# Nine unread products ahead of the first one, and input splits queued behind weight splits, in a hybrid SSM layer

## The chip, the cores and the metric

The kernel runs on one core of one Trainium2 chip. The metric is the device time of one execution in microseconds. Engines are named as in the profile: PE (TensorE, matmul), DVE (VectorE), ACT (ScalarE), POOL (GpSimd) and SP (SyncE, which issues most DMAs).

## The reference

One layer of a streaming encoder, for 256 prompt positions and 32 sample positions that share the weights. All data is f32.

```python
xn   = rmsnorm(x, norm_mix_pre)                  # x: 288 x 2048 in all
proj = xn @ w_in     # columns: u_pool 1024 | z 2048 | xBC 2560 | dt 32
pool = multi-scale trailing mean of u_pool, then a grouped product
ssd  = Mamba-2 mixer: causal conv on xBC, exact chunked scan, SiLU(z) gate, norm
x    = x + rmsnorm(concat[pool, ssd] @ w_out, norm_mix_post)
x    = x + rmsnorm(ConvFFN(rmsnorm(x, norm_ffn_pre)), norm_ffn_post)   # D_FF 5632
```

## The kernel before

The 288 positions are the columns of every product, and features lie on the 128 partitions. To get f32 accuracy from the faster f32r product, each operand is split into a high part (a copy rounded to f32r, on ACT) and a low part (the rest, on DVE). Each tile of 128 x 128 weights then costs three products, `mm3`: high weights by high input (L136), high weights by low input (L137), low weights by high input (L138).

The norm of the input is taken out of the product: the input is only scaled by the gain `g_mix_pre` while it is split (`split_from`, L99 on ACT and L100 on DVE), and `rstd` is multiplied in when the sums leave PSUM. `rstd` needs the sum of squares: ACT squares each input tile (L230 for the first, L233 into a `xsq` buffer for the others), POOL adds it to `xsum` (L234), and PE forms the mean with one product with the constant matrix `mean` (L242, into `prs`); ACT takes the root (L237) and DVE the reciprocal (L238).

The first stage runs over k, 16 steps of 128 input features. It forms 768 columns of `xBC` in six PSUM accumulators (five `acc`, one of the three `aux` banks), so a step is 6 x 3 = 18 products. Each step has one input split, one high weight split (L270, ACT) and one low weight split (L271, DVE). The weights come in DMAs of one or two steps from `w_first` into four `raw` buffers, and the split weights lie in four `whi` and four `wlo` buffers, so a split waits until PE has done with the step four earlier. SP issues the loads of input and weights in turn. After step 15 PE forms `dt` (`pdt`, L289), and the loops over the other `w_in` columns begin (`project`, with L130 and L131 as the weights' splits); there, DVE and ACT also do the convolutions and the scan, whose operands pass through DRAM (`xs_d`, `xw`, L450).

The order of instructions on an engine isn't written out: a scheduler places them by its own estimate of when each is ready, within the dependencies. `tc.keep_in_program_order` holds an instruction at its place in the program. `tc.issue_after(ins)` puts what is traced in its block behind `ins` on the engine of `ins`; it fixes the order of issue alone, and nothing waits for `ins` to end.

Of the kernel before, what the change touches and what calls it, by code (L numbers as in the profile page):

```python
# [8 lines left out]
F32 = mybir.dt.float32  # L9
F32R = mybir.dt.float32r  # L10
AF = mybir.ActivationFunctionType
# [5 lines left out]
P = 128  # L17
# [4 lines left out]
NT = NP_ + NS  # L22
# [21 lines left out]
def body(  # L44
# [26 lines left out]
    act, dve, pool, pe, sp = nc.scalar, nc.vector, nc.gpsimd, nc.tensor, nc.sync  # L71
# [11 lines left out]
    def aux(shape, name):  # L83
        return aux_ps.tile(shape, F32, tag="aux", name=name)

    def atile(name):
        return apool.tile([P, 2, NT], F32R, tag="a", name=name)
# [4 lines left out]
    def split_from(a, src, scale=None):  # L92

        if scale is None:
            act.activation(a[:, 0, :], src, AF.Copy)
            dve.tensor_tensor(a[:, 1, :], src, a[:, 0, :].bitcast(F32), op=ALU.subtract)
        else:
            return (
                act.activation(a[:, 0, :], src, AF.Copy, scale=scale),  # L99
                dve.scalar_tensor_tensor(  # L100
                    a[:, 1, :], src, scale, a[:, 0, :].bitcast(F32), op0=ALU.mult, op1=ALU.subtract
                ),
            )

    def wtile(part, n, nc_):

        t = wpool.tile([P, 1024 + 64], F32R, tag=part, name="w" + part)
        return t[:, 58 : 58 + n * nc_].rearrange("p (k c) -> p k c", k=n)
# [3 lines left out]
    def fetch_w(view, kb, nk, c0, nc_):  # L112
        raw = wpool.tile([P, nk, nc_], F32, tag="raw", name="raw")
        with tc.high_priority(offset=ahead[0]):
            sp.dma_start(out=raw, in_=view[:, c0 // 256, kb : kb + nk, :nc_])
        return raw
# [18 lines left out]
    def mm3(out, wh, wl, a, start, stop):  # L135
        pe.matmul(out, wh, a[:, 0, :], start=start, stop=False)  # L136
        pe.matmul(out, wh, a[:, 1, :], start=False, stop=False)  # L137
        pe.matmul(out, wl, a[:, 0, :], start=False, stop=stop)  # L138
# [43 lines left out]
    mean = const.tile([P, P], F32, name="mean")  # L182
# [29 lines left out]
    g_mix_pre = const.tile([P, KD], F32, name="g0")  # L212
# [5 lines left out]
    start = ExitStack()  # L218
    xin = start.enter_context(tc.tile_pool(name="xin", bufs=1))
    xT = xin.tile([P, KD, NT], F32, name="xT")  # L220
# [4 lines left out]
    def input_tiles(kb, n):  # L225
        sp.dma_start(out=xT[:, kb : kb + n, :], in_=x_in[:, kb : kb + n, :])

    def input_squares(k):
        if k == 0:
            act.activation(xsum, xT[:, k, :], AF.Square)  # L230
        else:
            q = xin.tile([P, NT], F32, tag="xsq", bufs=2, name="xsq")
            act.activation(q, xT[:, k, :], AF.Square)  # L233
            pool.tensor_tensor(xsum, xsum, q, op=ALU.add)  # L234

# [4 lines left out]
    def input_rstd():  # L240
        p_ = aux([P, NT], "prs")
        pe.matmul(p_, mean, xsum, start=True, stop=True)  # L242
        root(rstd, p_)

    act.dma_start(out=g_mix_pre, in_=g0_in)
    input_tiles(0, 1)
    first = [acc_ps.tile([P, NT], F32, tag="acc", name="acc") if m < 5 else aux([P, NT], "acc_x") for m in range(6)]
    chunks = ((0, 1), (1, 1)) + tuple((k, 2) for k in range(2, KD, 2))
    x_with = {0: (1, 1), 1: (2, 2), 2: (4, 2), 4: (6, 3), 6: (9, 3), 8: (12, 4)}
    for kb, n in chunks:  # L250
        raw = wpool.tile([P, n, 768], F32, tag="raw", name="raw")
        sp.dma_start(out=raw, in_=w_first[:, kb : kb + n, :])
        if kb in x_with:
            input_tiles(*x_with[kb])
        if kb == 1:
            pool.dma_start(out=wdt, in_=w_dt)
        if kb == 2:
            pool.dma_start(out=par1, in_=par1_in)
            pool.dma_start(out=hp, in_=hp_in)
        if kb == 6:  # L260
            pool.dma_start(out=pc, in_=par2_in[:, :120])
            pool.dma_start(out=pf, in_=par2_in[:, 120:].rearrange("p (r t) -> p r t", r=6))
        for k in range(kb, kb + n):
            a = atile("xn")
            split_from(a, xT[:, k, :], g_mix_pre[:, k : k + 1])
            xn.append(a)
            hi, lo = wtile("hi", 1, 768)[:, 0, :], wtile("lo", 1, 768)[:, 0, :]
            step = 256 if k == 0 else 768
            for c in range(0, 768, step):
                act.activation(hi[:, c : c + step], raw[:, k - kb, c : c + step], AF.Copy)  # L270
                dve.tensor_tensor(  # L271
                    lo[:, c : c + step], raw[:, k - kb, c : c + step], hi[:, c : c + step].bitcast(F32), op=ALU.subtract
                )
            for t in range(k - 1, k) if 0 < k < 9 else range(2 * k - 10, 2 * k - 8) if 8 < k < 13 else ():
                input_squares(t)
            if k == 13:
                input_rstd()
            for m in range(6):
                c = slice(m * P, (m + 1) * P)
                mm3(first[m], hi[:, c], lo[:, c], a, k == 0, k == KD - 1)  # L280
# [5 lines left out]
    for r in range(4):  # L286
        for q in range(4):
            k = 4 * q + r
# [287 lines left out]
    xT = op_.tile([P, KD, NT], F32, name="xT2")  # L576
# [68 lines left out]
    for t in range(NX):  # L645
        a = atile("mixs")
# [28 lines left out]
    for gi in range(2):  # L675
        c = slice(gi * P, (gi + 1) * P)
# [85 lines left out]
    for k in range(KD):  # L762
        if k % 2 == 0:
            raw = wpool.tile([P, 2, 896], F32, tag="raw", name="raw")
# [4 lines left out]
        a = atile("hn")  # L769
        hi = act.activation(a[:, 0, :], x1[k], AF.Copy, scale=g_ffn_pre[:, k : k + 1])  # L770
# [6 lines left out]
        else:  # L777
            q = op_.tile([P, NT], F32, tag="sq", bufs=2, name="sq")
# [11 lines left out]
        for m in range(7):  # L790
            c = slice(m * P, (m + 1) * P)
# [85 lines left out]
    for q in range(4):  # L877
        for b in range(2):
            t = apool.tile([P, 512], F32, tag="a", name="xr")
# [106 lines left out]
    for kb, n in ((0, K_RUN), (K_RUN, 8), (K_RUN + 8, 8)):  # L986
        raw = fetch_w(wd2, kb, n, (KD - 2) * P, 256)
# [3 lines left out]
        for piece in split_w(raw, kb, n, 256):  # L991
            for low in (True, False) if kb else (True,):
                for j in range(2):
                    c = slice(j * P, (j + 1) * P)
                    for k, hi, lo in piece:
                        a = f2[k]
# [8 lines left out]
    for j in range(2):  # L1005
        t = KD - 2 + j
# [4 lines left out]
    for j in range(2):  # L1011
        c = slice(j * P, (j + 1) * P)
# [108 lines left out]
```

## Time and profile before

| | |
|---|---|
| median of 3 runs | 1338.72 us (1338.0 to 1338.82) |
| profiled execution | 1337.7 us, span 1336.0 us |
| PE busy | 1312.7 us, 98% of the span |
| DVE busy | 887.1 us, 66% |
| ACT busy | 665.3 us, 50% |
| POOL busy | 239.8 us, 18% |
| mean granted TensorE clock | 0.996 |
| DMA | 249.82 MB, mean 187 GB/s |

In rows of the timeline the columns are start and duration in us, engine, line and operation, output and inputs, shapes, the number of instructions merged, and, in brackets, the engine's idle time before it with what ended it. Rows of the waits give total us, times and the longest wait. Rows of groups give the count, then busy us and mean ns of one, then idle time. Rows of the chain of work give start, duration and what. In a row of windows, the numbers behind the window are its length, the busy time of PE, weight loads, DVE, ACT and POOL (with counts), the granted clock, the share of DMA and GB/s.

### The profile page before, as it was taken

Reading aid. Unit: us, or ns where it says so; the run is one execution under the profiler, and the core shown is the slowest. Engines: PE = TensorE matmul, PEld = TensorE weight load, DVE = VectorE, ACT = ScalarE, POOL = GpSimd, SP = SyncE. Lnnn points to the kernel's source line nnn. Section 1 sums busy time; section 2 is a strip of 40 time slices with the busy share of each in tenths; the row PEclk is TensorE's granted clock in tenths of the full one; section 3 lists DMA queues with packets and bytes.
Section 4 is the critical chain, followed back from the end, with each engine's and each line's share of the span. In section 5 each row is a group of like instructions: output and inputs, shape, how many; then the busy total and the mean of one; then the engine's idle time right before and its main releaser. Section 6 shows DMA issues by size and latency. Waiting matters only on the chain.

```text
span 1336.0 us, 25101 instructions
## 1 busy us (share of the span) xinstructions
PE 1312.7 (98%) x10041; PEld 1297.0 (97%) x10041; DVE 887.1 (66%) x1437; ACT 665.3 (50%) x1002; POOL 239.8 (18%) x376
## 2 busy tenths in 40 slices
PE   7999999999999999999999999999999999999996
PEld 7999999999999989999999999999999999999996
DVE  7898998788544469977676644335666666664444
ACT  7558777446443455644445433334454444454442
POOL 6221102240212123211121100001111111101110
PEclk9999999999999999999999999999999999999998
DMA  7667884456656435766544544554544544566653
GB/s 285 230 194 258 280 248 150 152 207 216 238 205 205 146 121 189 208 180 187 179 158 164 176 146 170 174 182 159 181 166 158 174 174 158 168 239 175 208 177 94
DMA packets 104009, 249.82 MB, mean 187 GB/s; under 512 B 63748, under 2 KB 69444, under 8 KB 81492
## 3 DMA queue, kind: packets, MB, share of 16 engines
q1 hardware_dynamic: 101972, 243.11, 55.4%
q0 software_dynamic: 1488, 4.92, 1.1%
q8 instruction: 78, 1.28, 0.4%
q14 instruction: 39, 0.32, 0.1%
q10 hardware_dynamic: 432, 0.19, 0.1%
HBM read 236.23 MB, written 11.95 MB: 186 GB/s over the span
## 4 chain that ended last, share of the span: by engine, by line
PE 91%; DVE 3%; DMA 2%; issue 1%; POOL 1%; ACT 0%; SPq 0%; DVEq 0%; POOLq 0%; ACTq 0%
PE acc L138 30%; PE acc L136 29%; PE acc L137 29%; DMA xw<-xs_d 1%; POOL xs L640 1%; DMA raw<-in_w_first 1%; DVE xn L100 1%; PE py L467 1%; DMA xs_d<-blocks 1%; DVE wlo L271 0%; DVE xr L959 0%; PE acc_x L138 0%; PE run_a L1002 0%; PE acc_x L137 0%; DVE wlo L131 0%
## 5 line engine op out<-in xcount | busy, mean ns | idle before, releaser
L131 DVE TENSOR_TENSOR wlo<-raw,whi 128x1024 fp32r<-128x1024 f32 (+1 forms) x386 | 464.3, 1204 | 329.4 <-ACT whi L130 328.7
L130 ACT ACTIVATE whi<-raw 128x1024 fp32r<-128x1024 f32 (+1 forms) x386 | 399.3, 1036 | 471.9 <-PE acc L137 384.9
L138 PE MATMUL acc<-hn,wlo 128*128 128x288 f32 x1376 | 409.3, 298 | 0.0
L136 PE MATMUL acc<-hn,whi 128*128 128x288 f32 x1376 | 402.5, 293 | 0.5 <-ACT hn L770 0.5
L137 PE MATMUL acc<-hn,whi 128*128 128x288 f32 x1376 | 399.6, 291 | 1.2 <-DVE hn L771 1.2
L137 PEld LDWEIGHTS acc<-hn,whi 128*128 128x128 f32 x1376 | 258.9, 188 | 1.5 <-DVE hn L771 1.4
L136 PEld LDWEIGHTS acc<-hn,whi 128*128 128x128 f32 x1376 | 258.7, 188 | 1.3 <-ACT hn L770 1.3
L138 PEld LDWEIGHTS acc<-hn,wlo 128*128 128x128 f32 x1376 | 258.7, 188 | 0.0
L136 PE MATMUL acc<-xn,whi 128*128 128x288 f32 x688 | 203.8, 298 | 5.6 <-ACT whi L270 5.6
L137 PE MATMUL acc<-xn,whi 128*128 128x288 f32 x688 | 200.8, 293 | 0.0
L138 PE MATMUL acc<-xn,wlo 128*128 128x288 f32 x688 | 198.7, 298 | 1.6 <-DVE wlo L271 1.4
L138 PE MATMUL acc<-fa,wlo 128*128 128x288 f32 x660 | 196.4, 298 | 0.0
L136 PE MATMUL acc<-fa,whi 128*128 128x288 f32 x660 | 193.1, 293 | 0.0
L137 PE MATMUL acc<-fa,whi 128*128 128x288 f32 x660 | 191.4, 290 | 0.0
L136 PEld LDWEIGHTS acc<-xn,whi 128*128 128x128 f32 x688 | 130.3, 189 | 6.5 <-ACT whi L270 5.6
L137 PEld LDWEIGHTS acc<-xn,whi 128*128 128x128 f32 x688 | 130.3, 189 | 0.2
L138 PEld LDWEIGHTS acc<-xn,wlo 128*128 128x128 f32 x688 | 127.7, 189 | 2.6 <-DVE wlo L271 1.6
L137 PEld LDWEIGHTS acc<-fa,whi 128*128 128x128 f32 x660 | 123.9, 188 | 0.0
L136 PEld LDWEIGHTS acc<-fa,whi 128*128 128x128 f32 x660 | 123.9, 188 | 0.0
L138 PEld LDWEIGHTS acc<-fa,wlo 128*128 128x128 f32 x660 | 123.9, 188 | 0.0
L816 POOL COPY fc_stage<-ebuf 128x4 f32<-128x4 f32 x88 | 27.2, 309 | 466.8 <-DVE ebuf L815 466.8
L812 POOL COPY ebuf<-pf 128x2 f32<-128x2 f32 x88 | 67.4, 767 | 140.6 <-DVE fc L822 79.4
(279 smaller groups left out, 1716.1 us busy)
## 6 DMA issues: line engine op xcount, KB each, us to landing
raw<-in_w_up SPq DMA_DIRECT2D x80, 1024.0 KB, 4.8
raw<-in_w_in SPq DMA_DIRECT2D x38, 1024.0 KB, 5.4
raw<-in_w_down SPq DMA_DIRECT2D x32, 1024.0 KB, 4.8
raw<-in_w_out SPq DMA_DIRECT2D x24, 1024.0 KB, 4.8
raw<-in_w_down SPq DMA_DIRECT2D x16, 768.0 KB, 4.3
raw<-in_w_up SPq DMA_DIRECT2D x8, 896.0 KB, 4.5
gb<-g_d SPq DMA_DIRECT2D x8, 832.0 KB, 6.6
raw<-in_w_first SPq DMA_DIRECT2D x7, 768.0 KB, 10.2
```

Source lines behind the costliest of these rows:

```text
L100: dve.scalar_tensor_tensor(a[:, 1, :], src, scale, a[:, 0, :].bitcast(F32), op0=ALU.mult, op1=ALU.subtract),
L130: act.activation(hi, raw[:, k : k + n, :], AF.Copy)
L131: dve.tensor_tensor(lo, raw[:, k : k + n, :], hi.bitcast(F32), op=ALU.subtract)
L136: pe.matmul(out, wh, a[:, 0, :], start=start, stop=False)
L137: pe.matmul(out, wh, a[:, 1, :], start=False, stop=False)
L138: pe.matmul(out, wl, a[:, 0, :], start=False, stop=stop)
L467: pe.matmul(y[:, 0:256], xw[:, 0, c], m[:, j, 0:256], start=True, stop=False)
L640: pool.tensor_tensor(xs[t], xs[t], rg[1], op=ALU.mult)
L812: pool.tensor_copy(e[:, 258:260], pf[:, 4:6, i])
L816: pool.tensor_copy(fc_stage[:, :, :, i], e[:, 256:324].rearrange("p (s c) -> p s c", c=34)[:, :, 0:2])
```

## The change

Nine products of `mean` by `mean` into an `aux` bank that nothing reads are placed ahead of the first product, held in program order. The split of the input of step k is queued behind the two weight splits of step k - 2 on their engines, from step 3 on; the squares that belong to step k are queued behind the high weight split of step k - 1 on ACT. The `xsq` buffers become four instead of two, and the mean's product with `rstd` moves from step 13 to step 14.

```diff
-            q = xin.tile([P, NT], F32, tag="xsq", bufs=2, name="xsq")
+            q = xin.tile([P, NT], F32, tag="xsq", bufs=4, name="xsq")
...
     input_tiles(0, 1)
+    cut = []
+    idle = aux([P, P], "idle")
+    for i in range(9):
+        tc.keep_in_program_order(pe.matmul(idle, mean, mean, start=True, stop=True))
...
             a = atile("xn")
-            split_from(a, xT[:, k, :], g_mix_pre[:, k : k + 1])
+            with ExitStack() as order:
+                for ins in cut[k - 2] if k > 2 else ():
+                    order.enter_context(tc.issue_after(ins.ins))
+                split_from(a, xT[:, k, :], g_mix_pre[:, k : k + 1])
...
             for c in range(0, 768, step):
-                act.activation(hi[:, c : c + step], raw[:, k - kb, c : c + step], AF.Copy)
-                dve.tensor_tensor(
+                w_hi = act.activation(hi[:, c : c + step], raw[:, k - kb, c : c + step], AF.Copy)
+                w_lo = dve.tensor_tensor(
                     lo[:, c : c + step], raw[:, k - kb, c : c + step], hi[:, c : c + step].bitcast(F32), op=ALU.subtract
                 )
+            cut.append((w_hi, w_lo))
             for t in range(k - 1, k) if 0 < k < 9 else range(2 * k - 10, 2 * k - 8) if 8 < k < 13 else ():
-                input_squares(t)
-            if k == 13:
+                with tc.issue_after(cut[k - 1][0].ins):
+                    input_squares(t)
+            if k == 14:
                 input_rstd()
```

In the changed program the lines behind the edits move by a few: L270 and L271 become L277 and L278, L289 becomes L298.

## The prediction

> **What bounds the kernel now.** I read the page's head first, then the waits of PE, then the first 50 us along the chain and the timeline of each engine, because both edits lie in the first stage.
>
> ```profile
> span 1336.0 us, 25101 instructions
> PE 1312.7 (98%) x10041; PEld 1297.0 (97%) x10041; DVE 887.1 (66%) x1437; ACT 665.3 (50%) x1002; POOL 239.8 (18%) x376
> ```
> ```profile
> PE acc L136 <- ACT whi L270: 5.6, 1, 5.6
> ...
> PE acc L138 <- DVE wlo L271: 1.4, 1, 1.4
> ...
> PE acc L138 <- DVE wlo L131: 0.2, 1, 0.2
> ```
>
> PE is busy for 98% of the span, so time can only come from PE's few gaps and from products that run slowly. Two gaps lie in the first stage: 5.6 us before the first product, and 1.4 us on a low split (L271). A third loss is no wait, so only the distances between products show it.
>
> ```profile
> 5.55 0.61 PE L136 MATMUL acc<-xn,whi 128*128 128x288 f32 x1 [5.55 <-ACT whi L270]
> ...
> 10.04 0.44 PE L136 MATMUL acc<-xn,whi 128*128 128x288 f32 x1
> 10.28 0.44 PE L137 MATMUL acc<-xn,whi 128*128 128x288 f32 x1
> ...
> 11.23 0.30 PE L137 MATMUL acc<-xn,whi 128*128 128x288 f32 x1
> ...
> 15.35 0.29 PE L136 MATMUL acc<-xn,whi 128*128 128x288 f32 x1
> ...
> 17.73 0.30 PE L136 MATMUL acc<-xn,whi 128*128 128x288 f32 x1
> ...
> 20.13 0.30 PE L136 MATMUL acc<-xn,whi 128*128 128x288 f32 x1
> ```
> ```profile
> 0.00:10.00 10.00, 4.45 (x18) 4.45 (x19) 4.35 (x9) 6.17 (x13) 7.23 (x39) 1.00 0.80 267
> ```
>
> 15.35, 17.73 and 20.13 are the starts of steps 3, 4 and 5: a step of 18 products takes 2.39 us, 0.13 for one. Up to about 11.05 equal products start 0.24 us apart (10.04 to 10.28), although the granted clock of the window, 1.00 ahead of the row's last two numbers, shows no brake. So PE takes 5.5 us from its first product, 5.55, to reach full pace.
>
> **The nine products.** They read only `mean`, ready early on POOL, and write one PSUM bank that nobody reads.
>
> ```profile
> 0.95 0.21 POOL L183 MEMSET mean<- 128x128 f32 x1
> ```
> ```profile
> 40.99 0.48 PE prs L242 x2
> 3.16 7.42 DMA raw<-in_w_first
> 10.60 0.85 ACT whi L270
> ```
>
> The trace holds no such product. The nearest is `prs`, also a plain f32 product with `mean`, 288 columns, 0.48 us at full pace. By columns, 128/288 x 0.48 = 0.21 us; at the slow pace (0.24/0.13) 0.39 us; nine take 3.5 us, from about 1.3 (the memset ends at 1.16) to 4.8. That is free: PE has nothing before 5.55. The other bound is a product that does not shrink with its columns, 0.48 x 0.24/0.13 = 0.89 us, nine to 9.3. I take 3.5: what `prs` costs at full pace is 3.7 times one of the 0.13 us products of equal width, so columns set its price. By the long bound steps 0 and 1 (4.8 us at full pace) end at 14.1 instead of 11.45, and 2.6 of the sum below is lost; the range keeps it.
>
> If PE is at full pace by 5.55, step 0 ends at 5.55 + 2.39 = 7.94 and step 1 at 10.33. Step 2 cannot start then: its weights come by the DMA that lands at 10.58 and a high split of 0.85 us, so at 11.45. The lead saved is therefore not all 24 slow products x 0.11 = 2.6 us. Step 4 starts at 11.45 + 2 x 2.39 = 16.23 instead of 17.73: **1.50 us**. This is forgiving: with full pace only from a time t, every microsecond that t lies behind 5.55 makes step 1 end 0.45 us later (1 - 0.13/0.24), so up to t = 8.0 nothing is lost. By the same 5.5 us as before, counted from the first of the nine, t is 1.3 + 5.5 = 6.8.
>
> [...]
>
> **The order of the first stage.** `issue_after` is order on one engine, no semaphore: in the changed order no instruction of L99, L100, L230 or L233 has a new wait, and ACT's squares may run four ahead of POOL's adds instead of two.
>
> ```profile
> 18.15 4.32 DVE L100 SCALAR_TENSOR_TENSOR xn<-xT,g,xn 128x288 fp32r<-128x288 f32 x6
> 22.42 3.02 DVE L271 TENSOR_TENSOR wlo<-raw,whi 128x768 fp32r<-128x768 f32 x2
> 25.36 3.54 DVE L100 SCALAR_TENSOR_TENSOR xn<-xT,g,xn 128x288 fp32r<-128x288 f32 x4
> 28.82 5.63 DVE L271 TENSOR_TENSOR wlo<-raw,whi 128x768 fp32r<-128x768 f32 x5
> ```
> ```profile
> 28.77 0.29 PE L137 MATMUL acc_x<-xn,whi 128*128 128x288 f32 x1
> 30.43 0.93 PE L138 MATMUL acc<-xn,wlo 128*128 128x288 f32 x5 [1.36 <-DVE wlo L271]
> 31.20 0.30 PE L138 MATMUL acc_x<-xn,wlo 128*128 128x288 f32 x1
> 31.33 0.30 PE L136 MATMUL acc<-xn,whi 128*128 128x288 f32 x1
> ```
> ```profile
> L271 DVE TENSOR_TENSOR wlo<-raw,whi 128x768 fp32r<-128x768 f32 x9 | 11.1, 1282 | 0.0
> L100 DVE SCALAR_TENSOR_TENSOR xn<-xT,g,xn 128x288 fp32r<-128x288 f32 x12 | 9.9, 883 | 0.0
> ```
>
> ```profile
> L271 DVE TENSOR_TENSOR wlo<-raw,whi 128x768 fp32r<-128x768 f32 x3 | 2.9, 960 | 3.0 <-ACT whi L270 3.0
> ```
> ```profile
> 12.36 0.68 DVE wdt L284
> ```
>
> Of these groups the first two are from 13.5 to 33 us, the third from the quiet 34.5 to 41. DVE does six and then four input splits (L100) ahead of weight splits that PE needs sooner, and PE stands from 28.90 (28.77 + 0.13) to 30.43: **1.53 us**. In the changed order at most two input splits stand before two low splits. Is DVE then in time everywhere, with PE 1.5 us earlier? In the crowded window it took 9.9/12 + 11.1/9 = 0.83 + 1.23 = 2.06 us for a step, against 2.39 of PE. From the high split at 11.45 it does the low split of step 2 (0.96), the `wdt` product (0.68) and the low split of step 3 (1.28), to about 14.4; then the low split of an even step k, behind two input splits, is done at 14.4 + 2.06(k - 4) + 2.9, and PE, after 12 products of the step, wants it at 16.23 + 2.39(k - 4) + 12 x 0.13: 17.3 against 17.8 for step 4, 21.4 against 22.6 for step 6, 25.5 against 27.4 for step 8. The thinnest cover is 0.5 us, at step 4. Loads only gain: the buffers of later weights are freed by low splits, which come earlier.
>
> The mean's product and `rstd` move one step later (k 14), past ACT's high splits, its table load and DVE's reciprocal:
>
> ```profile
> 41.97 1.28 ACT L237 ACT_TABLE_LOAD   x1
> 43.80 1.95 DVE L238 RECIPROCAL rstd<-rstd 128x288 f32<-128x288 f32 x1 [0.59 <-ACT rstd L237]
> ...
> 47.08 0.18 DVE L327 TENSOR_TENSOR ebuf<-acc,rstd 128x32 f32<-128x32 f32 x1
> 48.49 2.15 PE L289 MATMUL pdt<-xT,wdt 128*32 128x288 f32 x32
> ```
>
> PE comes to it at 11.45 + 12 x 2.39 = 40.1, 0.9 us sooner than now (40.99). From there the trace has 1.0 us to the table load, 3.8 to the reciprocal's end (45.75) and 1.5 to the first freed bank (47.26): the bank is free at 46.4. PE ends step 15 at 11.45 + 14 x 2.39 + 0.5 = 45.4 and the 2.1 us of `pdt` at 47.5, so nothing waits, with 1.1 us of cover. The sum of squares must be done by 40.1; its 15 adds begin earlier than now. The unread bank is one of three `aux` banks; `pdt` takes it next, long after.
>
> **After the first stage.** Is the lead kept? DVE and ACT only come 1 to 2 us earlier, not 3. But they are ahead of PE soon after:
>
> ```profile
> 83.03 1.06 ACT L130 ACTIVATE whi<-raw 128x1024 fp32r<-128x1024 f32 x1 [1.04 <-PE acc L137]
> 86.17 1.06 ACT L130 ACTIVATE whi<-raw 128x1024 fp32r<-128x1024 f32 x1 [2.08 <-PE acc L137]
> ```
>
> There the high splits wait for PE to free a buffer, 3.14 us apart, which is PE's pace: the lead passes through. Later it is thin:
>
> ```profile
> 142.37 1.21 DVE L131 TENSOR_TENSOR wlo<-raw,whi 128x1024 fp32r<-128x1024 f32 x1
> ...
> 178.28 0.96 DVE L450 TENSOR_TENSOR xw<-xw,tok 128x768 f32<-128x768 f32 x1 [0.99 <-DMA xw<-xs_d]
> 179.16 1.22 DVE L131 TENSOR_TENSOR wlo<-raw,whi 128x1024 fp32r<-128x1024 f32 x1
> ```
> ```profile
> 144.40 0.29 PE L138 MATMUL acc<-xn,wlo 128*128 128x288 f32 x1
> ```
>
> The split that ends at 143.58 is read at 144.40, 0.82 us later, and the one of 179.16 is the late one of 0.2 us. The changed program orders this region anew (PE's order is the same again from about 180 on), with slightly less DVE work ahead of most of these splits, and the `xw` product no longer directly ahead of the one at 179.16. I count nothing; bounds: 0.4 gained there, or 1.0 lost.
>
> **Sum.** 1.50 + 1.53 = 3.03 us. The profiled execution took 1337.7 (span 1336.0 and 1.7 around it) and would take 1334.7; the median of the runs is 1.0 above it, so **1335.7** from 1338.72.
>
> **Rivals.** *The clock is not raised early*: the gap from 4.8 to 5.55 starts the count again, and t stays 11.05. Then step 4 starts at 17.73 as now and only the stall goes: 1338.72 - 1.53 = 1337.2. For it: the trace has only unbroken work ahead of the change of pace, 5.5 us of it. Against: PE would be busy for 3.5 of the 4.2 us before its first real product, and 0.75 us of rest is short beside 5.5; the 1.4 us stand at 29 did not slow the products after it (31.20 to 31.33). [...]
>
> *The low splits stay late*: the stall moves to step 4 or 6, where cover is 0.5 to 1.2 us. For it: a low split took 1.28 us in the crowded window and 0.96 in the quiet one; what differs is POOL's adds, and with four square buffers these come earlier and closer together. Were each DVE operation slowed by as much again (0.32 us), a step would cost DVE 2.06 + 0.64 = 2.70 against 2.39: step 4 is 0.5 late and each of the next four 0.3 more, 1.7 given back, 1337.4. Against it: the sum takes the crowded price already, and the number of adds is the same. [...]
>
> *Slower, the mixer's new order*: in the loop over `w_in` columns, DVE holds the weights' splits behind `xw` products that wait for a DMA.
>
> ```profile
> DVE xw L450 <- DMA xw<-xs_d: 6.0, 4, 2.2
> ```
>
> Four waits of up to 2.2 us cost PE next to nothing now. Where a new place puts each directly ahead of a split with 0.8 us of cover, one costs 1.4. Six such products lie before 180: five so placed cost 7.0, less 3.0, +4.0, 1342.7. It is slower at all from three on (4.2 against 3.0), by over 0.2% from five. Against it: the new order has three of the six one or two splits later than now, so their DMAs have longer to land.
>
> **How the numbers follow.** Forecast 0.58, of which 0.07 falls short of 0.2% (2.7 us, about what a measurement of this kernel tells from no change); more than forecast, by later gaps closing too, 0.06; clock 0.15; late splits 0.10; slower 0.11. Faster: 0.51 + 0.06 = 0.57; same: 0.07 + 0.15 + 0.10 = 0.32; slower 0.11. The range runs from 1334.7 (another 1.0 gained) to 1338.3 (all but 0.4 of the gain gone, as by the long bound of the nine products, or one rival's 1337.2 or 1337.4 and 1.0 lost in the mixer).
>
> **What would show it.** Right: the nine products (line 250 of the changed program) end by 5.5; products of steps 0 and 1 are 0.13 apart by 8; PE waits about 1.1 us near 10.4 on the high split of step 2; no wait on L271 later; `pdt` starts near 45.4, and the group waiting at 179 comes 3 us earlier. Wrong: distances of 0.24 beyond 9, a wait on a low split between 16 and 24, or waits of PE on L131's low splits between 100 and 180 above 1 us in all.

## The result and the profile after

The changed kernel takes 1334.22 us (median of 8 runs, 1332.74 to 1334.81); beside it the kernel before took 1337.57 (8 runs, 1336.96 to 1338.82). The ratio is 0.9974, 95% interval 0.9964 to 0.9984: 3.35 us faster, where 3.02 were forecast from 1338.72. The direction and the size of the gain came as forecast; the time itself lies 0.5 us below the range.

The head of the page of after, and the waits of PE (total us, times, longest):

```profile
span 1332.1 us, 25141 instructions
PE 1316.2 (99%) x10059; PEld 1300.6 (98%) x10059; DVE 886.4 (67%) x1437; ACT 666.5 (50%) x1002; POOL 247.6 (19%) x376
```
```profile
PE acc L136 <- ACT du L95: 1.9, 1, 1.9
PE acc L137 <- DVE hn L780: 1.2, 1, 1.2
PE idle L250 <- POOL mean L183: 1.2, 1, 1.2
...
PE psum_t L806 <- POOL xsum L789: 0.6, 1, 0.6
...
PE acc L136 <- ACT whi L277: 0.2, 1, 0.2
```

PE's opening wait of 5.6 us is now 1.2, and the wait of 1.4 us on a low split is gone. One more row had another size before:

```profile
PE psum_t L797 <- POOL xsum L780: 2.2, 1, 2.2
```

The start on PE's timeline:

```profile
1.21 4.21 PE L250 MATMUL idle<-mean 128*128 128x128 f32 x18 [1.21 <-POOL mean L183]
5.27 0.61 PE L136 MATMUL acc<-xn,whi 128*128 128x288 f32 x1
...
6.88 0.37 PE L136 MATMUL acc<-xn,whi 128*128 128x288 f32 x1
7.09 0.29 PE L137 MATMUL acc<-xn,whi 128*128 128x288 f32 x1
...
10.00 0.29 PE L137 MATMUL acc_x<-xn,whi 128*128 128x288 f32 x1
...
11.24 0.40 PE L136 MATMUL acc<-xn,whi 128*128 128x288 f32 x1 [0.16 <-ACT whi L277]
...
16.12 0.29 PE L136 MATMUL acc<-xn,whi 128*128 128x288 f32 x1
```
```profile
45.28 2.15 PE L298 MATMUL pdt<-xT,wdt 128*32 128x288 f32 x32
```

The nine products (18 records) run from 1.21 to 5.27, 0.45 us each; full pace comes at 7.09, step 2 starts at 11.24, step 4 at 16.12 (17.73 before) and `pdt` at 45.28 (48.49).

With the start times of the same products in both traces, the lead of after over before can be followed along PE: 1.61 us at step 4, 3.26 at 31, 3.36 at 135, 3.85 from 182 to 286, 2.32 from 300 to 487, 0.78 from 490 to 522, 2.34 up to 526, 3.90 at the end. The drops behind 287 and 487 and the recovery behind 520 are not the edits' doing: the same changed kernel, run again as both_again, has none of the drops (3.48 at 286, 3.38 from 300 to 524). They are stretches in which PE runs at half clock; the rows of five and of four windows (the granted clock is the number ahead of the last two), after first, then before:

```profile
283.52:286.94 3.42, 1.51 (x12) 1.50 (x12) 3.38 (x7) 1.40 (x2) 1.40 (x3) 1.00 0.17 69
286.94:290.35 3.41, 3.41 (x16) 3.41 (x15) 3.41 (x11) 0.44 (x1) 0.99 (x3) 0.50 0.71 226
290.35:293.76 3.41, 3.41 (x27) 3.41 (x27) 3.41 (x10) 1.39 (x2) 1.31 (x1) 1.00 0.20 84
```
```profile
481.50:484.91 3.41, 1.75 (x10) 1.33 (x10) 3.24 (x7) 2.13 (x6) 1.17 (x1) 1.00 0.40 152
484.91:488.33 3.42, 3.42 (x16) 3.42 (x15) 3.08 (x4) 3.29 (x7) 2.11 (x2) 0.50 0.01 2
```
```profile
523.21:526.62 3.41, 1.50 (x9) 1.40 (x10) 3.41 (x5) 2.96 (x5) 1.04 (x1) 1.00 0.67 271
526.62:530.03 3.41, 3.41 (x17) 3.41 (x16) 3.41 (x4) 1.06 (x1) 0.00 (x0) 0.50 0.79 252
287.69:291.10 3.41, 1.81 (x13) 1.81 (x14) 3.38 (x7) 1.40 (x2) 1.09 (x2) 1.00 0.04 17
291.10:294.51 3.41, 3.41 (x28) 3.41 (x27) 3.41 (x12) 0.68 (x2) 1.00 (x3) 1.00 0.83 262
```

A stretch at 0.5 lasts 3.41 us and costs some 1.55 us (1.53, 1.54 and 1.56 in the leads above). The profile of before has one, behind the rest at `psum_t`; that of after has one behind the rest at `du` and one from 484.9, behind two rests on `hn`, that the wait at `psum_t` takes up (0.6 us instead of 2.2). The rest at `du` is the same 1.9 us in both kernels, and only in after it was followed by half clock. That is the first thing the experiments had to explain; the second was whether the two edits give what the prediction ascribed to each.

### The profile page after: what moved, and what is told of

Its sections match the earlier page's. It is cut to its first block, busy times and chain, and to the rows that moved or that the text cites. A ratio compares the mean times of both kernels' runs of the same rounds, so it can differ in the third digit from the quotient of the medians.

```text
span 1332.1 us, 25141 instructions
## 1 busy us (share of the span) xinstructions
PE 1316.2 (99%) x10059; PEld 1300.6 (98%) x10059; DVE 886.4 (67%) x1437; ACT 666.5 (50%) x1002; POOL 247.6 (19%) x376
## 3 DMA queue, kind: packets, MB, share of 16 engines
q8 instruction: 78, 1.28, 0.4%
## 4 chain that ended last, share of the span: by engine, by line
PE 93%; DVE 3%; issue 1%; POOL 1%; DMA 1%; ACT 0%; SPq 0%; DVEq 0%; POOLq 0%; ACTq 0%
PE acc L136 30%; PE acc L138 30%; PE acc L137 30%; DVE wlo L798 1%; DVE mg L767 1%; POOL xs L649 1%; DVE hn L780 1%; PE py L476 1%; DMA raw<-in_w_first 1%; DVE xr L968 0%; PE run_a L1011 0%; PE low L1009 0%; PE py L478 0%; PE pst L711 0%; PE acc_x L138 0%
## 5 line engine op out<-in xcount | busy, mean ns | idle before, releaser
L138 PE MATMUL acc<-hn,wlo 128*128 128x288 f32 x1376 | 402.9, 293 | 0.0
L138 PE MATMUL acc<-xn,wlo 128*128 128x288 f32 x688 | 195.4, 296 | 0.0
L138 PE MATMUL acc<-fa,wlo 128*128 128x288 f32 x660 | 193.1, 293 | 0.0
L831 DVE SCALAR_TENSOR_TENSOR fc<-ebuf,pf,fc 128x290 f32<-128x290 f32 x176 | 90.2, 518 | 2.6
```

What stands on the lines that cost most here:

```text
L831: dve.scalar_tensor_tensor(c, e[:, r_ : r_ + 290], pf[:, r_, i : i + 1], c, op0=ALU.mult, op1=ALU.add)
```

## The experiments

All times are medians against the kernel before on the same chip, which took 1337.08, 1337.30, 1337.03 and 1337.37 in the four sets below.

### Each half of the change alone

Left out of the change, in turn: the order edit (nine_only), the nine products (order_only); then the whole change again, and the change with four products.

```diff
 nine_only, on the kernel before:
+    idle = aux([P, P], "idle")
+    for i in range(9):
+        tc.keep_in_program_order(pe.matmul(idle, mean, mean, start=True, stop=True))
 order_only, on the changed kernel: the same lines taken out
 idle_4, on the changed kernel:
-    for i in range(9):
+    for i in range(4):
```

> The nine unread products alone, the first stage's order as before. Theory (the two parts are not independent): full pace is reached near 7 us and step 4 starts near 16.1 instead of 17.7, but DVE's order and speed are unchanged, so the low split that PE waits for ends at about 30.4 as before; PE only waits there for about 3.1 us instead of 1.5, pdt starts near 48.4 and the time is that of before within 0.3 us. Rival (the parts add): the lead of 1.6 us is kept, pdt starts near 46.9, 1.6 us faster than before.

> The changed order of the first stage (splits and squares bound, four square buffers, the mean's product at step 14) without the nine products. Theory: full pace only near 11 us, step 4 starts near 17.7 as before, no wait on a low split later, pdt starts near 46.9; 1.6 us faster than before, up to 0.6 more where the new order in the mixer closes the small waits at 135 and 180. Rival (the order needs the lead, or only the lead counts): a low split is late again and less than 0.5 us is gained.

> The changed kernel once more, beside the two halves: 3.3 us faster than before, pdt near 45.3. If the two halves above were additive, their gains would sum to this; by the theory of dependent parts nine_only gives nothing and order_only 1.6 to 2.2, so 1.1 to 1.7 comes from the pair alone.

> The changed kernel with four unread products instead of nine. They end near 3.0 us and PE rests 2.3 us before the first real product at 5.3. Theory (what releases the clock is a stretch of time that is busy for the most part): the rest is too long, full pace comes 5.5 us after the first real product, near 10.9, step 4 starts near 17.5 and about 1.5 us of the gain is lost (1335.7 where the changed kernel has 1334.2). Rival (the first product starts a fixed count of 5.5 us, rest or no rest): full pace near 6.9 and the same time as with nine.

| | median | ratio to before |
|---|---|---|
| nine_only | 1336.91 | 1.0000 (0.9991 to 1.0008) |
| order_only | 1334.94 | 0.9978 (0.9969 to 0.9986) |
| both_again | 1333.91 | 0.9977 (0.9966 to 0.9987) |
| idle_4 | 1335.24 | 0.9981 (0.9972 to 0.9991) |

The parts do not simply add: the nine alone bring nothing that these runs can tell (the interval is 1.2 us to either side). Their trace, on PE, shows where the lead goes:

```profile
22.89 0.40 PE L136 MATMUL acc<-xn,whi 128*128 128x288 f32 x1 [1.09 <-ACT whi L273]
...
30.88 0.94 PE L138 MATMUL acc<-xn,wlo 128*128 128x288 f32 x5 [1.34 <-DVE wlo L274]
```

0.9 us ahead of before at step 4, PE then waits on a high split near 23 and on the low split as before near 30, and is 0.45 behind at 31: DVE and ACT set the pace there, so coming sooner only means waiting longer.

The clock at the start was the surprise. Order_only has no unread product, and still reached full pace at 8.3, not near 11:

```profile
7.86 0.44 PE L136 MATMUL acc<-xn,whi 128*128 128x288 f32 x1
8.10 0.38 PE L137 MATMUL acc<-xn,whi 128*128 128x288 f32 x1
8.32 0.29 PE L136 MATMUL acc_x<-xn,whi 128*128 128x288 f32 x1
```

Its first product started at 5.29, so this is 3.0 us after it, where the kernel before took 5.7. Idle_4 (first unread product at 1.21) reached it at 8.6, not by either theory's 10.9 or 6.9. No fixed count of busy time fits 3.0 and 5.7. A grid does: in every trace the record of the granted clock begins at the change of pace, and each stretch at 0.5 begins a whole number of 3.413 us later (151 of them in before, 82 in after). So in these traces the clock changes at the ends of windows of 3.413 us, and these lie differently relative to the kernel's start in each execution: the same kernel reached full pace at 7.0 in after and at 5.5 in both_again, 1.5 apart. With the ends of those windows and PE's idle time in each, the 18 profiles of this study sort like this:

- A window that was idle for 0.5 us or less released full pace (before order_only's change of pace: 0.43 idle); one idle for 0.9 or more did not. The two between fall on either side (0.59 released, 0.56 did not).
- A window idle for 1.91 us or more was followed by half clock (7 of 7); none idle for 1.87 or less at `du` or `psum_t` was. The window near 480, with its two rests on `hn`, did it at 1.65 (4 of 4) and not at 1.54. So idle time as the profile shows it is not the whole rule; what differs near 480 stays open.

So what the nine products buy is a better chance of an early start at full pace. The lead over the profile of before, which with 11.21 had the latest of all:

| squares bound | nine | full pace at | lead at step 4 | lead at 31 us |
|---|---|---|---|---|
| no | no: before, before_fill | 11.2, 10.6 | 0, 0.27 | 0, -0.02 |
| no | yes: nine_only, nine_fill | 4.0, 4.2 | 0.88, 1.28 | -0.45, -0.37 |
| yes | no: order_only, squares_only, squares_fill | 8.3, 8.5, 9.7 | 1.46, 0.96, 0.33 | 3.12, 2.58, 2.02 |
| yes | yes: after, both_again, squares_bound, fill_four, fill_gaps, nine_squares_fill | 7.0, 5.5, 5.5, 5.5, 4.3, 10.6 | 1.61, 1.27, 1.65, 1.26, 1.35, 0.05 | 3.26, 2.92, 3.27, 2.91, 3.01, 1.70 |

(The kernels named here for the first time follow below.) With the stall in place no lead of the start reaches 31 us, that of the nine or that of chance. Without it every lead does, with 1.6 to 1.7 us more. That is why the parts don't add, and the likely reason why the order edit alone brings 2.1 and not 1.6: it also lets through what chance gives at the start, 0.92 at step 4 on average over its three profiles. The six with the nine have 1.20 there, so the nine are worth 0.3 us, and up to 0.7 with the other profiles without them counted in (0.51 over seven); not 1.50. One profile even shows the prediction's rival. In it the nine were issued as always, but the rest behind them lay in the wrong window:

```profile
5.97 0.61 PE L136 MATMUL acc<-xn,whi 128*128 128x288 f32 x1 [0.56 <-ACT whi L274]
...
10.22 0.44 PE L138 MATMUL acc_x<-xn,wlo 128*128 128x288 f32 x1
10.46 0.35 PE L136 MATMUL acc<-xn,whi 128*128 128x288 f32 x1
10.64 0.29 PE L137 MATMUL acc<-xn,whi 128*128 128x288 f32 x1
```

For the rests further on, 1.91 us in one window, 56% of it, was enough for half clock (after at `du`, before at `psum_t`), and 1.72 to 1.87 (50 to 55%) at `du` or `psum_t` was not.

### More of the nine, and the halves of the order edit

```diff
 idle_18, on the changed kernel:
-    for i in range(9):
+    for i in range(18):
 splits_bound, on the changed kernel (squares free, two buffers, rstd at 13):
-                with tc.issue_after(cut[k - 1][0].ins):
-                    input_squares(t)
-            if k == 14:
+                input_squares(t)
+            if k == 13:
 squares_bound, on the changed kernel (input splits free):
-            with ExitStack() as order:
-                for ins in cut[k - 2] if k > 2 else ():
-                    order.enter_context(tc.issue_after(ins.ins))
-                split_from(a, xT[:, k, :], g_mix_pre[:, k : k + 1])
+            split_from(a, xT[:, k, :], g_mix_pre[:, k : k + 1])
```

> Eighteen unread products instead of nine. Clock theory (windows of 3.41 us that run free of the kernel, full pace after the first one that is nearly all busy, so 2.8 to 6.2 us after the first unread product): the products cost 0.45 us each until then and about 0.23 after, and end between 6.7 and 8.4. Steps 0 and 1 follow at full pace and end between 11.5 and 13.2, later than the load of step 2 allows (11.2): step 4 starts between 16.3 and 18.0 and 0.2 to 1.9 us of the gain are given back, so about 1335 where the pair gives 1333.9. Rival (the products keep their first price whatever the clock): they end at 9.3, step 4 starts at 18.9, 2.8 us are given back, 1336.7. Second rival (products that nobody reads cost nothing): 1333.9.

> The change with the input's splits bound behind the weights' splits, but the squares free as before (two square buffers, reciprocal root at step 13). Theory (only the order of the splits on VectorE carries the gain): no wait on a low split in the first stage, lead from 31 us on within 0.4 us of the pair's, about 1334. Rival (the squares' place on ScalarE matters as much, because the high splits stand behind them): a wait of 1 us or more on a high or low split between 16 and 32, about 1335.5.

> The change with the squares bound, four square buffers and the later reciprocal root, but the input's splits free as before. Theory: six and then four input splits again stand ahead of weight splits on VectorE, so the wait on a low split near 29 us stays, at 1.5 us or longer since TensorE comes to it earlier; little is left of the gain, about 1336.5. Rival (the squares were what held the high splits up): no such wait, about 1334.

Idle_18 took 1334.09 (0.9977, 0.9968 to 0.9986), the same as the pair. In its profile full pace came at 4.4, step 0 started at 6.8, and step 4 0.77 us before 17.73: 0.5 later than the pair's repeat, little enough to vanish in the scatter.

The halves came out against the expectation. Splits_bound: 1336.30 (0.9991, 0.9982 to 1.0000), most of the gain gone: from step 4 to 31 us its lead grows by 0.68 us where after's grows by 1.65, and another 0.8 is lost near 130, ahead of a product `py`, for which the trace shows no cause. Squares_bound: 1333.66 (0.9974, 0.9965 to 0.9983), the whole of it, with DVE's input splits six and four in a row as before. In splits_bound the wait on a low split is gone too, as the prediction's reason has it, but PE waits on a high split instead, because ACT's squares, ahead of it, wait for POOL to give back one of two buffers (PE's timeline, then ACT's waits up to 50 us):

```profile
21.83 0.40 PE L136 MATMUL acc<-xn,whi 128*128 128x288 f32 x1 [0.71 <-ACT whi L277]
```
```profile
ACT xsq L233 <- POOL xsum L234: 3.5, 4, 1.6
```

In squares_bound DVE does the same sequence as before in less time. Its timeline, and below it POOL's:

```profile
17.28 3.76 DVE L100 SCALAR_TENSOR_TENSOR xn<-xT,g,xn 128x288 fp32r<-128x288 f32 x6
20.97 1.82 DVE L275 TENSOR_TENSOR wlo<-raw,whi 128x768 fp32r<-128x768 f32 x2
22.70 2.91 DVE L100 SCALAR_TENSOR_TENSOR xn<-xT,g,xn 128x288 fp32r<-128x288 f32 x4
```
```profile
21.45 2.01 POOL L234 TENSOR_TENSOR xsum<-xsum,xsq 128x288 f32<-128x288 f32 x1 [2.00 <-ACT xsq L233]
```

Before, the three groups took 4.32, 3.02 and 3.54 us: 2.4 us more for the same twelve instructions. What had changed beside them is POOL's adds of squares: before, nine begin in that time, here five, and the one above took 2.01 us (before, they take 0.8 to 1.1) while the two low splits beside it took 0.95 each. The means of the groups hide that a split on DVE has one of two prices here. Before, the first three of the six input splits, which begin before a row of adds at 19.09, and the next three, beside those adds, are:

```profile
L100 DVE SCALAR_TENSOR_TENSOR xn<-xT,g,xn 128x288 fp32r<-128x288 f32 x3 | 1.4, 505 | 0.0
L100 DVE SCALAR_TENSOR_TENSOR xn<-xT,g,xn 128x288 fp32r<-128x288 f32 x3 | 3.0, 1061 | 0.0
```

Low splits likewise take 0.95 or some 1.55 us. Eight of the twelve instructions paid the higher price before, four in squares_bound; at 0.55 to 0.6 us each that is about the 2.4. That gave a new theory: DVE was late because POOL's adds stretch its operations.

### The price of the adds

```diff
 no_adds, on the kernel before:
-            pool.tensor_tensor(xsum, xsum, q, op=ALU.add)
+            if k == KD - 1:
+                pool.tensor_tensor(xsum, xsum, q, op=ALU.add)
 squares_only, on the kernel before: the binding of the squares, four buffers, rstd at 14
 four_buffers, on the kernel before:
-            q = xin.tile([P, NT], F32, tag="xsq", bufs=2, name="xsq")
+            q = xin.tile([P, NT], F32, tag="xsq", bufs=4, name="xsq")
```

> The kernel before with fourteen of the fifteen adds of squares on GpSimd left out (only the last stays, so the sum of squares and with it the scale are wrong); VectorE's order is the same instruction for instruction. Theory now (VectorE was late near 29 us because GpSimd's adds stretch its operations, about 0.5 us each, not because of the order of the splits): the six input splits from 18 us take about 3.0 us instead of 4.32, the two low splits after them about 1.9 instead of 3.02, and the wait of TensorE on a low split is gone; 1.5 to 2.1 us less, about 1335.2. Rival (the prediction's reason: the order, input splits ahead of low splits): the wait stays at 1 us or more, time within 0.6 us of before.

> The kernel before with the squares bound behind the previous step's high split, four square buffers and the later reciprocal root; no unread products, input splits free as before. Theory: this alone is the whole gain of the first stage's order: no wait on a low split, 2.1 us less, about 1335.1, the same as the whole order edit without the nine products. Rival (the binding needs the lead of the nine products, or the splits' order, to bear fruit): wait of 1 us or more near 29, about 1337.

> The kernel before with four square buffers instead of two and nothing else. Theory (what counts is that GpSimd's adds come later than the stretch in which VectorE does its input splits, which only the binding does): with four buffers the squares and adds come as early as before or earlier, VectorE's six input splits from 18 us take 4 us or more, the wait on a low split stays at 1.2 us or more; time within 0.7 us of before. Rival (the buffers alone free the high splits on ScalarE): the wait falls below 0.5 us, about 1335.5.

DVE's groups from 11 to 31 us, first of the kernel before, then of no_adds (count, busy us, mean ns, idle time):

```profile
L271 DVE TENSOR_TENSOR wlo<-raw,whi 128x768 fp32r<-128x768 f32 x8 | 10.4, 1325 | 1.9 <-ACT whi L270 1.9
L100 DVE SCALAR_TENSOR_TENSOR xn<-xT,g,xn 128x288 fp32r<-128x288 f32 x12 | 9.9, 883 | 0.0
```
```profile
L272 DVE TENSOR_TENSOR wlo<-raw,whi 128x768 fp32r<-128x768 f32 x11 | 10.6, 1004 | 4.3 <-ACT whi L271 4.3
L100 DVE SCALAR_TENSOR_TENSOR xn<-xT,g,xn 128x288 fp32r<-128x288 f32 x12 | 5.6, 513 | 0.5 <-ACT xn L99 0.5
```

With the order of DVE unchanged, an input split falls from 883 to 513 ns on average and a low split from 1325 to 1004, DVE has 4.8 us to spare where it had 1.9, and PE's wait on the low split is gone: 1334.53 us (0.9979, 0.9970 to 0.9987). ACT's squares no longer wait for POOL in this kernel either, but in before DVE was busy without a break from 20 to 30 us, so what counted there is the length of its own operations. So the stall of 1.5 us needed both: input splits ahead of low splits, and adds beside them. In these traces either of the two engines paid: in squares_bound the add of 2.01 us lies beside two low splits that kept their 0.95.

Squares_only gives 1333.10 (0.9972, 0.9962 to 0.9982): the binding of the squares, with its four buffers and the later `rstd`, is the whole gain of the order edit, without the nine and without bound splits. The later `rstd` was not tried alone. Four_buffers shows that it is not the buffers: its adds run without a break from 18.6 and the six input splits take longer than before,

```profile
18.07 4.88 DVE L100 SCALAR_TENSOR_TENSOR xn<-xT,g,xn 128x288 fp32r<-128x288 f32 x6
```

as expected. The wait I expected with it cannot be read off, since the scheduler put `prs` and `pdt` into that place. The time was missed: 1341.36 (1.0039, 1.0023 to 1.0054; four runs), 4 us slower than before. With `pdt` so early the order of the mixer changed, which is the likely reason: in its profile a lead of 1.56 us at 48 is a lag of 1.50 at 200. Which of the mixer's steps costs how much was not followed up.

### Filling later rests

If a window with some 1.9 us of rest in it brings half clock, then unread products in the rest should keep it off. Fill_gaps puts seven ahead of the first product with `du` and eight ahead of `psum_t`; fill_four puts four in each place.

```diff
             c = slice(j * P, (j + 1) * P)
+            if i == 3 and j == 0:
+                for _ in range(7):
+                    pe.matmul(o[:, :P], mean, mean, start=True, stop=True)
...
+            if k == 13 and m == 1:
+                p_ = aux([P, NT], "psum_t")
+                with tc.issue_after(w_end.ins):
+                    for _ in range(8):
+                        pe.matmul(p_[:, :P], mean, mean, start=True, stop=True)
```

> The changed kernel with unread products also in two later rests of TensorE: seven ahead of the first product with du (a rest of 1.9 us near 284) and eight ahead of the product psum_t (2.2 us near 520); neither is filled whole, and the products that wait are not made later. Theory (after a window of 3.41 us that is idle for more than about half, the next window runs at half clock and costs 1.5 us; whether a rest of 1.9 us falls into one window is chance, so each run loses 0, 1.5 or 3 us): no stretch of the granted clock at 0.5 after these two rests, median 1.0 to 2.0 us lower than the pair's, near 1332.5, and the runs closer together (within 2 us where the pair's span 5). Rival (the half stretches come from something else, such as power): stretches stay, median within 0.5 of the pair's 1333.9 or, if the products delay what follows, above.

> The changed kernel with four unread products in each of two later rests of TensorE (ahead of du near 284 and of psum_t near 520), about 0.9 us in rests of 1.9 and 2.2 us; ScalarE, GpSimd and the queues keep their order and six instructions of VectorE move by a few places. Clock theory (a window of 3.41 us that is idle for over half brings one window at half clock, 1.5 us): no stretch at 0.5 after these two rests, no wait that was not there, median 1.0 to 1.8 us under the pair's 1333.9, the runs within 3 us of each other. Rival (rests do not bring the half stretches): they stay, and the median is that of the pair within 0.5 us.

Fill_gaps is slower: 1339.67 (1.0017, 1.0008 to 1.0026). Its fills moved instructions of ACT and DVE as well, and PE waits 3.7 us for one of them behind `psum_t`:

```profile
PE acc L136 <- DVE ebuf L831: 3.7, 1, 3.7
```

The clock did what the windows say all the same: 1.00 behind both filled rests, and half clock for two windows on end, 6.83 us, behind the new rest. With four products ACT, POOL and the queues keep their order and six instructions of DVE move by a few places; PE's rests fall from 1.9 to 1.0 and from 2.2 to 1.5. Fill_four took 1332.81 (0.9972, 0.9960 to 0.9983) in runs that lie between 1332.29 and 1332.99, and its windows around the two rests show no half clock:

```profile
279.00:292.00 13.00, 11.97 (x91) 11.65 (x90) 12.93 (x25) 3.97 (x5) 7.30 (x10) 1.00 0.63 236
519.00:532.00 13.00, 11.54 (x87) 11.25 (x86) 9.15 (x12) 5.92 (x8) 1.24 (x3) 1.00 0.83 280
```

But squares_only, unfilled, lay just as close (1332.68 to 1333.36), so a quiet set can come by chance. The last set puts the same fill of four on the kernel before and on three of the variants.

> The kernel before with four unread products in each of the two later rests (ahead of du near 290 and of psum_t near 525), nothing else. Clock theory: the half-clock stretches after these rests are where most of the runs' spread and about 1.5 us of the median come from, also in the kernel before: no stretch at 0.5 after the start, median 1.0 to 2.0 us lower, about 1335.6, the runs within 2 us of each other where those of before span 5 and more. Rival (the spread has another cause, the fill only happened to fall on quiet runs): span of runs over 3 us, median within 0.5 of before.

> The same fill on the kernel with the nine early products alone (no order edit). Theory: without the chance stretches the nine alone show what they bring: nothing, because the lead of up to 1.5 us is lost to the waits on a high split near 23 and a low split near 30; within 0.5 us of the filled kernel before, 1335.6 (0.9 at most to either side). Rival (the parts add, the noise hid it): 0.9 to 1.5 us under the filled kernel before.

> The same fill on the kernel with the squares bound alone (no early products, no bound splits). Theory: 2.2 to 2.7 us under the filled kernel before, about 1333.1, and not lower than squares bound without the fill where that had no stretches (1332.7 to 1333.4).

> The same fill, with nine early products and bound squares (splits free). Theory of free-running windows: without the nine, full pace comes 2.8 to 6.2 us after the first product near 5.4, so at 8.2 to 11.6, and each us beyond 8.0 costs 0.45: 0.1 to 1.6, by chance; with them none. So 0.4 to 1.0 us under the squares alone with fill, about 1332.4, and the lowest median of all. Rival (a lead of the first 12 us is given back later): equal to the squares alone within 0.3.

| | median | runs | ratio to before |
|---|---|---|---|
| before_fill | 1336.32 | 1335.55 to 1338.32 | 0.9994 (0.9985 to 1.0004) |
| nine_fill | 1336.50 | 1335.77 to 1338.49 | 0.9992 (0.9983 to 1.0001) |
| squares_fill | 1333.72 | 1333.19 to 1335.25 | 0.9972 (0.9962 to 0.9982) |
| nine_squares_fill | 1333.04 | 1332.47 to 1333.96 | 0.9965 (0.9952 to 0.9978) |

None of the five profiles with a fill of four has half clock behind `du` or `psum_t`; of the twelve without any fill, six have it there. (Nine_squares_fill has one from 485.0, behind the unfilled rests on `hn`.) Chance alone would give none of five about once in 13 times, but in those five no window at the two rests is idle for more than 1.43 us, and the mean granted clock, on record for every run of the four sets, bears it out: a stretch lowers it by 0.0013 (0.5 x 3.41 / 1336), and 0.995 or less stands in none of the 42 runs with a fill of four, in 30 of the 100 of the variants without fill, and in 24 of the 111 of before. The same record ties the clock to the time: the runs of before at 0.995 take 1338.1 us on average (24 runs), those at 0.997 1336.4 (44 runs).

The runs of before_fill lie within 2.8 us where those of before beside them (25 runs, against 11) span 5.7, and the median is 1.05 lower. The interval still holds no change, and squares_fill has the ratio of squares_only, 0.9972. So the effect on the clock is shown; that on the median is likely, not shown. Nor is all scatter the clock's: the runs of before_fill at 0.997 still lie between 1336.30 and 1338.32, and the cause is open. Nine_fill equals before_fill, so the nine alone bring nothing also with the half clock behind the two rests taken out. On top of the bound squares they bring 0.68, near what the windows allow, but the two intervals overlap.

## Why the prediction was right or wrong

**Missed: the time and its range, through the anchor.** The sum was 3.03 us, measured 3.35. But it was taken from 1338.72, the median of three runs, and the same kernel took 1337.0 to 1337.6 in five sets of 8 to 34 runs; the set of 8 holds those three, and its other five lie between 1336.96 and 1337.66. From 1337.57 the same sum gives 1334.5, 0.3 from what was measured. The failing step is the sum's "the median of the runs is 1.0 above it", carried to the new kernel as if it were a constant. In the five sets the median is not above the profiled execution's 1337.7 at all, but 0.1 to 0.7 below it. The 1.0 was scatter of three runs, and scatter of this kernel comes in part from half clock behind none, one or two of its rests (1336.4 us at a mean granted clock of 0.997, 1338.1 at 0.995). The low end of the range let 1.0 be gained in the mixer and gave nothing to the anchor.

**The nine products: right in mechanism, wrong in size on average.** They took 0.45 us each, not 0.39, and ended at 5.27, inside the cover. Full pace at 7.09 against a forecast of 6.8, step 2 at 11.24 against 11.45, step 4 at 16.12 against 16.23: in this profile the step is right to 0.2 us (1.61 against 1.50). That it came so close is luck: the six profiles with the nine and the bound squares have 0.05 to 1.65. The wait of about 1.1 us near 10.4 that was to show it is 0.16 us at 11.2, because with full pace at 7.09 PE is through step 1 only by 11.1, so little of the cover was left. And "by the same 5.5 us as before" is no constant of the chip: 2.8 to 5.9 us occurred, 7.4 with four products and 9.3 once with nine, by the phase of the windows, and over the profiles the nine are worth 0.3 to 0.7; the rest of the step was there to be had by chance, once the stall was gone. The rival that the rest restarts the count is real, in one profile of those with the nine.

**The order of the first stage: right in size, wrong in which half does it.** 1.53 was forecast; the lead grows from 1.61 to 3.26. The reason given, input splits ahead of low splits, is one of two causes: bound splits alone remove that wait and make another of 0.71 us on a high split, and bound squares alone remove it and make none. The step that failed is "the number of adds is the same", with which the rival about POOL's adds was set aside: the number is the same, but not their time, and an input split takes 0.51 us or, held up beside an add, 1.06 (883 ns on average with the adds and 513 without). The prediction's crowded price of 1.28 us for a low split was such an average, of splits of 0.95 and of some 1.55 us.

**The scale one step later: right.** `pdt` starts at 45.28 against 45.4, with no wait.

**After the first stage: the lead passes whole, as counted.** The 0.1 us near 135 and 0.5 near 180 that came on top are not the change's: before_fill, whose first fill lies near 287, gained the same 0.11 and 0.50 there over the first profile of before (PE's wait on the low split near 180 is in that profile and not in this one).

**Together, in the profiles:** 1.61 + 1.65 = 3.26 us of the edits at 31, against 3.03 forecast; 0.6 by chance up to 286; then 1.5 lost behind `du`, 1.5 lost on `hn` and won back by the shorter wait at `psum_t`, and 1.6 won behind `psum_t`, where before has its stretch: 3.9. Over the six profiles with both, the lead at 31 is 2.84 on average, and that of the order before does not hang on its start (0 and -0.02), so the sum of 3.03 holds. Its division does not: three profiles of the order edit without the nine have 2.57 of it. That a first half which is too large and a chance lead which was left out come so near to the sum is luck.

## What to carry to other kernels

Before a median of a few runs becomes the anchor of a forecast, look in its profile for stretches at half clock and for rests of TensorE that could bring one (here 1.91 us in one window of 3.41): they come and go between executions of the same program, and here two of them (3.1 us by the price of 1.55 each) are worth about as much as the change. Where VectorE is late, ask what GpSimd does beside it before asking for another order: here a split held up beside an add took 0.55 to 0.6 us longer, and moving the adds, by the binding of the squares with its buffers and the later `rstd`, did what the whole edit did, and the bound splits were not needed. Work that nobody reads, put ahead of the first product, pays only as far as the engines that feed the next steps can follow (here no lead at 31 us with the stall in place, 0.3 to 0.7 us without it), which must be shown with the other stall gone.

## What the runs showed of the hardware that was not expected

In these traces the granted clock changes on a grid of 3.413 us (151 steps of it between two changes in before, 82 in after) whose phase differs from one execution to the next. A window with 1.91 us of rest in it was followed by 3.41 us at half clock, which cost some 1.55 us; the same rest at `du` in before, divided over two windows as 0.31 and 1.60 us, was followed by full clock. With the two rests at `du` and `psum_t`, half clock moves one execution against another by up to 3.1 us, an estimate from twice 1.55. Four plain f32 products of 128 x 128 x 128 in each rest kept it off in all five profiles, and in none of 42 runs was the mean granted clock 0.995 or less. The start at half pace (products 0.24 us apart, later 0.13) is not in the window's clock column, which reads 1.00 there. Beside GpSimd's adds, an input split or a low split on VectorE either kept its time or took 0.55 to 0.6 us longer (0.51 or 1.06 us at 128 x 288, 0.95 or 1.55 at 128 x 768), and at times the add paid instead, once (squares_bound) 2.01 us where the kernel before has 0.8 to 1.1.
